# One-core hybrid decoder block: PSUM banks of scores and transposes, the first weight transfer, and the place of the diagonal products

## The chip, the core and the metric

The kernel runs on one core of a Trainium2 chip. The metric is the device time of one execution in microseconds (us); the time given for a kernel is the median of several runs. Engines are named as the profile names them: PE (TensorE matmul), PEld (TensorE weight load), DVE (VectorE), ACT (ScalarE), POOL (GpSimd), SP (SyncE, which here only issues DMAs).

## What is computed

For x of 256 tokens by 1024 channels the reference computes one decoder block:

```python
h = rmsnorm(x, attn_norm_g)
hq, hf, hi, hg, aq, ak, av, gl = split(h @ w_in)          # 1024 x 9216
y_hg = hgrn2_mix(hq, hf, hi, hg, lb, hg_out_norm_g) @ w_branch_hg
att  = moba_attention(rmsnorm(aq), rmsnorm(ak), av, rel_bias_table)
y_at = att @ w_branch_attn
merged = sigmoid(gl[0]) * y_hg + sigmoid(gl[1]) * y_at
x = x + merged @ w_out
h2 = rmsnorm(x, ffn_norm_g)
x = x + (silu(h2 @ w_ffn_gate) * (h2 @ w_ffn_up)) @ w_ffn_down
```

With 256 tokens and blocks of 256 the attention is plain causal attention of 8 heads of 128 with a relative bias. The recurrence (8 heads of 128) is computed by the kernel as a masked product of queries and decayed keys.

## The kernel before, in words

**Precision.** Each large product is made from three matmuls in the type fp32r: an operand is split into a high part (`whi`, cast on ACT, L55) and a remainder (`wlo`, subtraction on DVE, L56), and the kernel sums high x high, high x low and low x high (L81 to L83, L98 to L101, L608 to L610). So each weight tile needs a DMA issued by SP (L64), an ACT cast and a DVE subtraction before PE can use both parts. Transposes, scores and the products of the recurrence are in plain fp32.

**Start (L116 to L161).** The first product, V0, is the first half of the recurrence's values. Its weights and x come in seven pieces, one k-tile of 128 rows each and two in the last. For a piece, ACT casts the weights (L146), DVE or ACT multiplies x by the norm gain held in `vec` (L150 for the first k-tile, L152 for the others), DVE makes the two remainders (L153, L155), and PE does six matmuls per k-tile (L160). Before: the weights of the first k-tile (256 KB) and then `vec` (17.5 KB) are issued by ACT (L120, L121), all the other transfers by SP, of which x of the first k-tile (128 KB) leads (L122). The eight matmuls of L129 on a tile of ones run in the meantime.

**Blocks.** `feat_block` (L86) and `tok_block` (L76) make 512 output columns each, from two chunks of four k-tiles of weights. Three buffers of `wraw`, `whi` and `wlo` turn round; SP issues the next load when DVE has read a `wraw` for the last time.

**PSUM.** There are eight banks in three groups: `pw` has four (the blocks), `pa` two, `ph` two. Before the change, the transposes in `head_T` (L424 to L434) and the scores (L450 to L461) take `pa` alone. The recurrence's levels (L322) take `ph`, and so do its diagonal products (L309).

**Attention and recurrence (L498 to L535).** They are written interleaved: a block of k or q, then one level of the recurrence, and so on. A level (`hgrn_level`) is an ACT copy (L320), a group of small matmuls into one `ph` bank (L332), four predicated copies out of it on DVE (L338) and DVE products (L349, L351) that the next level needs. `hgrn_diag` (L297) makes three passes over 128x2048 elements on DVE (L301, L302, L56) and a cast on ACT (L55); `hgrn_diag_put` (L306) multiplies the result by ones on PE and puts it on the diagonal of A.

**What sets the order.** Program order is only a priority: when the program is built, a planner places the instructions of each engine by it and by its own model of when operands and buffers are ready, and the engine then runs that fixed order. This can be seen in the trace, where pieces of a level (L332) stand between the transposes of `head_T` (L431), which come before it in the program.

Of the kernel before, what the change touches and what calls it, by code (L numbers as in the profile page):

```python
# [14 lines left out]
P = 128  # L15
# [12 lines left out]
def tile_hgrn2_moba_block(ctx: ExitStack, tc: tile.TileContext, xm, xT, vecs, table, onehot,  # L28
                          w_in, w_hg, w_at, w_out, w_gate, w_up, w_down, out):
    nc = tc.nc  # L30
# [10 lines left out]
    def ph(name="ph"):  # L41
        return psum.tile([P, 512], F32, name=name, tag="ph", bufs=2)

    def pa(name="pa"):
        return psum.tile([P, 512], F32, name=name, tag="pa", bufs=2)
# [8 lines left out]
    def split(src, hi, lo):  # L54
        nc.scalar.copy(hi, src)  # L55
        nc.vector.tensor_sub(lo, src, hi.bitcast(F32))  # L56
# [19 lines left out]
    def tok_block(w, c0, act, parts=(4, 4), bank=pw):  # L76
        ps = [bank(), bank()]
        for kt, wh, wl in chunks(w, c0, 512, parts):
            for tb in range(2):
                ts = slice(tb * P, (tb + 1) * P)  # L80
                nc.tensor.matmul(ps[tb], part(act, kt, 0)[:, ts], wh, start=(kt == 0), stop=False)  # L81
                nc.tensor.matmul(ps[tb], part(act, kt, 0)[:, ts], wl, start=False, stop=False)  # L82
                nc.tensor.matmul(ps[tb], part(act, kt, 1)[:, ts], wh, start=False, stop=(kt == KT - 1))  # L83
        return ps
# [32 lines left out]
    xTr = big.tile([P, KT, S], F32, name="xTr", tag="T1")  # L117
    XT = [big.tile([P, 4, 2, S], F32R, name=f"XT{i}", tag=("XH", "XL")[i]) for i in range(2)]
    raws = [wp.tile([P, 4, 512], F32, name="wraw") for _ in range(2)]
    nc.scalar.dma_start(raws[0][:, 0, :], w_in[0:P, 2048:2560])  # L120
    nc.scalar.dma_start(vec, vecs)  # L121
    nc.sync.dma_start(xTr[:, 0:1, :], xT[:, 0:1, :])  # L122
    ones = const.tile([P, P], F32, name="ones")
    nc.vector.memset(ones, 1.0)
# [55 lines left out]
    def rinv(dst, ss, n):  # L180
        nc.vector.tensor_scalar(dst, ss, 1.0 / n, EPS, op0=OP.mult, op1=OP.add)
        nc.scalar.activation(dst, dst, AF.Sqrt)
        nc.vector.reciprocal(dst, dst)
# [41 lines left out]
    def put_tok(dst, ps, half):  # L225
        for tb in range(2):
            nc.scalar.mul(dst[:, tb, half * 512:(half + 1) * 512], ps[tb], rx[:, tb:tb + 1])
# [31 lines left out]
    bank = pa()  # L259
# [37 lines left out]
    def hgrn_diag():  # L297
        qk = big.tile([P, 2, H, P], F32, name="qk", tag="T9")
        qkh = big.tile([P, 2, H, P], F32R, name="qkh", tag="T10")
        qkl = big.tile([P, 2, H, P], F32R, name="qkl", tag="T8")  # L300
        nc.vector.tensor_mul(qk, Q, K)  # L301
        nc.vector.tensor_mul(QA, Q, Fg)  # L302
        split(qk, qkh, qkl)
        return qkh, qkl

    def hgrn_diag_put(qkh, qkl):  # L306
        for tb in range(2):
            for g in range(2):
                bank = ph().rearrange("p (h t) -> p h t", h=4)  # L309
                for m, part in enumerate((qkh, qkl)):  # L310
                    nc.tensor.matmul(bank, ones_r, part[:, tb, 4 * g:4 * g + 4, :], start=(m == 0), stop=(m == 1))
                nc.vector.tensor_mul(A[:, tb, 4 * g:4 * g + 4, :], bank,
                                     ident.unsqueeze(1).to_broadcast([P, 4, P]))
# [103 lines left out]
    def qk_block(tok, sq, c0, half, bank=pw):  # L417
        put_tok(tok, tok_block(w_in, c0 + half * 512, XT, bank=bank), half)
        for tb in range(2):
            for h in range(half * 4, half * 4 + 4):  # L420
                jk = small.tile([P, P], F32, name="jk")
                nc.scalar.activation(jk, tok[:, tb, h * P:(h + 1) * P], AF.Square, accum_out=sq[:, tb, h:h + 1])

    def head_T(tok, tag, nm, gain):  # L424
        tT = big.tile([P, H, S], F32, name=nm, tag=tag)
        for g in range(4):
            bank = pa()
            for i in range(2):
                for tb in range(2):
                    h = 2 * g + i  # L430
                    nc.tensor.transpose(bank[:, i * S + tb * P:i * S + (tb + 1) * P],  # L431
                                        tok[:, tb, h * P:(h + 1) * P], ident)
            nc.scalar.mul(tT[:, 2 * g:2 * g + 2, :].rearrange("p h t -> p (h t)"), bank, gain)
        return tT  # L434

    def keys(ktok, kss):
        rk = small.tile([P, 2, H], F32, name="rk")
        rinv(rk, kss, P)
        for tb in range(2):
            kv = ktok[:, tb, :].rearrange("p (h d) -> p h d", h=H)  # L440
            nc.vector.tensor_mul(kv, kv, rk[:, tb, :].unsqueeze(2).to_broadcast([P, H, P]))
        return head_T(ktok, "T9", "kT", kg)

    def scores(qtok, qss, kT):
        rq = small.tile([P, 2, H], F32, name="rq")
        rinv(rq, qss, P)
        qT = head_T(qtok, "T10", "qT", qg[:, 0:1])
        S0 = big.tile([P, H, P], F32, name="S0", tag="T13")
        S1 = big.tile([P, H, S], F32, name="S1", tag="T7")
        for sc, tb, w, bt in ((S0, 0, P, B0), (S1, 1, S, B1)):  # L450
            m = 512 // w
            for g in range(H // m):
                bank = pa()
                for i in range(m):
                    h = m * g + i
                    nc.tensor.matmul(bank[:, i * w:(i + 1) * w], qT[:, h, tb * P:(tb + 1) * P], kT[:, h, 0:w],  # L456
                                     start=True, stop=True)
                for i in range(m):
                    h = m * g + i
                    nc.vector.scalar_tensor_tensor(sc[:, h, :], bank[:, i * w:(i + 1) * w], rq[:, tb, h:h + 1],  # L460
                                                   bt[:, h, :], op0=OP.mult, op1=OP.add)  # L461
        return S0, S1
# [35 lines left out]
    ktok = big.tile([P, 2, D], F32, name="ktok", tag="T7")  # L498
    kss = small.tile([P, 2, H], F32, name="kss")
    qk_block(ktok, kss, 5120, 0, bank=pa)  # L500
    qkd = hgrn_diag()
    qk_block(ktok, kss, 5120, 1)
    hgrn_diag_put(*qkd)
    hgrn_level(0)
    qtok = big.tile([P, 2, D], F32, name="qtok", tag="T8")
# [5 lines left out]
    hgrn_level(2)  # L511
    put_tok(V, tok_block(w_in, 2048 + 512, XT), 1)
    S0, S1 = scores(qtok, qss, kT)
    hgrn_level(3)
    Va = big.tile([P, 2, D], F32, name="Va", tag="T8")
# [37 lines left out]
    for half in range(2):  # L553
# [5 lines left out]
        for tb in range(2):  # L559
            g = G[0][:, tb, hs]  # L560
            nc.vector.tensor_mul(g, g, ps[tb])
            nc.vector.tensor_add(g, g, G[1][:, tb, hs])
            bank = ph()
# [8 lines left out]
    for half in range(2):  # L572
        ps = tok_block(w_out, half * 512, M)
        for tb in range(2):
            xs = x2[:, tb, half * 512:(half + 1) * 512]
            nc.vector.tensor_add(xs, xs, ps[tb])
            bank = ph()
# [110 lines left out]
```

## Time and profile before

| | us |
|---|---|
| median of 3 runs | 508.66 |
| lowest and highest | 508.34, 509.21 |
| profiled execution | 509.63 |
| span of its records | 507.6 |
| PE busy in it | 499.4 (98%) |

The profile is of one execution, which took 509.63 us; its engine records span 507.6 us, so 2.03 us lie outside of them. Times in rows are counted from the start of the span. In a timeline row the first number is the start, the second the length, then come the engine, the line, the operation, the tiles and the count; brackets name what ended an idle time before the row. Consecutive matmuls overlap in the records, so the distance between starts is what a matmul costs the engine.

### The profile page before, as it was taken

The page shows a single profiled execution, that of the slowest core. Times are in us where ns is not written, and L with a number is a line of the kernel's source. Part 1 is how long each engine was busy: PE and PEld are TensorE (multiplying, and loading weights), DVE is VectorE, ACT ScalarE, POOL GpSimd, SP SyncE. Part 2 cuts the span into 40 slices and gives each one's busy share as a digit, 9 for nine tenths or more (in the row PEclk, how much of TensorE's full clock was granted, in tenths as well). Part 3 has the DMA queues.
Part 4 walks back from the last instruction along what each step waited for, and adds up shares of the span by engine and source line. Part 5 has one row for each costly group of instructions (what it writes and reads, how often), then busy time and mean ns, then how long its engine had stood idle before and what let it go on. Part 6 is the DMA issues. An engine that isn't in the chain of part 4 may idle for free.

```text
span 507.6 us, 6636 instructions
## 1 busy us (share of the span) xinstructions
PE 499.4 (98%) x2674; PEld 419.4 (83%) x2674; DVE 332.7 (66%) x380; ACT 283.3 (56%) x418; POOL 21.3 (4%) x41
## 2 busy tenths in 40 slices
PE   7999999999999999999999999999999999999996
PEld 6878887788888888888888888888888888888885
DVE  5669998887599643373456577867655746566372
ACT  5497566777658656955434334665535535544350
POOL 9201300000000000000000000000000000000000
PEclk9999999999999999999999999999999999999999
DMA  8956956524523642276556555556655655653522
GB/s 245 388 178 193 338 197 224 190 83 167 167 70 112 235 166 86 80 252 224 188 168 221 187 170 166 167 175 201 203 167 175 212 194 169 202 169 90 190 94 83
DMA packets 44126, 91.20 MB, mean 180 GB/s; under 512 B 1944, under 2 KB 5048, under 8 KB 44096
## 3 DMA queue, kind: packets, MB, share of 16 engines
q1 hardware_dynamic: 43072, 87.86, 51.8%
q0 software_dynamic: 736, 2.65, 1.7%
q8 instruction: 21, 0.34, 0.3%
q10 hardware_dynamic: 288, 0.28, 0.2%
q14 instruction: 9, 0.07, 0.0%
HBM read 89.70 MB, written 1.07 MB: 179 GB/s over the span
## 4 chain that ended last, share of the span: by engine, by line
PE 95%; ACT 2%; DMA 1%; DVE 1%; issue 0%; DVEq 0%; ACTq 0%
PE pw L99 21%; PE pw L81 13%; PE pw L82 13%; PE pw L83 13%; PE pw L98 9%; PE acc L608 4%; PE acc L609 4%; PE acc L610 4%; PE pw L160 3%; PE ph L332 2%; PE pw L101 1%; PE pa L456 1%; DMA vec<-vecs 1%; PE ph L382 1%; PE pa L492 1%; PE pa L81 1%
## 5 line engine op out<-in xcount | busy, mean ns | idle before, releaser
L56 DVE TENSOR_TENSOR wlo<-wraw,whi 128x2048 fp32r<-128x2048 f32 (+1 forms) x83 | 182.2, 2197 | 113.6 <-ACT whi L55 113.2
L55 ACT CAST whi<-wraw 128x2048 fp32r<-128x2048 f32 (+1 forms) x83 | 151.7, 1829 | 114.4 <-PE pw L83 52.7
L99 PE MATMUL pw<-x2T,whi 128*128 128x512 f32 x352 | 121.8, 398 | 0.0
L98 PE MATMUL pw<-x2T,wlo 128*128 128x256 f32 x308 | 86.5, 281 | 0.0
L81 PE MATMUL pw<-whi,XT 128*128 128x512 f32 x192 | 76.0, 396 | 0.0
L82 PE MATMUL pw<-wlo,XT 128*128 128x512 f32 x192 | 75.4, 392 | 0.6 <-DVE wlo L56 0.6
L83 PE MATMUL pw<-whi,XT 128*128 128x512 f32 x192 | 75.2, 392 | 0.0
L99 PEld LDWEIGHTS pw<-x2T,whi 128*128 128x128 f32 x352 | 63.4, 188 | 12.4
L98 PEld LDWEIGHTS pw<-x2T,wlo 128*128 128x128 f32 x308 | 58.2, 189 | 1.8
L99 PE MATMUL pw<-XT,whi 128*128 128x512 f32 x128 | 44.5, 399 | 0.2 <-DVE Fg L111 0.2
L82 PEld LDWEIGHTS pw<-wlo,XT 128*128 128x128 f32 x192 | 36.1, 188 | 8.2 <-DVE wlo L56 1.0
L81 PEld LDWEIGHTS pw<-whi,XT 128*128 128x128 f32 x192 | 36.1, 188 | 7.5
L83 PEld LDWEIGHTS pw<-whi,XT 128*128 128x128 f32 x192 | 36.1, 188 | 7.4
L608 PE MATMUL acc<-whi,hT 128*128 128x512 f32 x88 | 34.3, 390 | 0.0
L610 PE MATMUL acc<-whi,hT 128*128 128x512 f32 x88 | 34.3, 389 | 0.0
L609 PE MATMUL acc<-wlo,hT 128*128 128x512 f32 x88 | 34.2, 389 | 0.0
L98 PE MATMUL pw<-XT,wlo 128*128 128x256 f32 x112 | 31.4, 280 | 0.0
L99 PEld LDWEIGHTS pw<-XT,whi 128*128 128x128 f32 x128 | 23.3, 188 | 5.1 <-DVE Fg L111 0.5
L98 PEld LDWEIGHTS pw<-XT,wlo 128*128 128x128 f32 x112 | 21.1, 189 | 0.6
L610 PEld LDWEIGHTS acc<-whi,hT 128*128 128x128 f32 x88 | 16.5, 188 | 3.5
L609 PEld LDWEIGHTS acc<-wlo,hT 128*128 128x128 f32 x88 | 16.5, 188 | 3.5
L608 PEld LDWEIGHTS acc<-whi,hT 128*128 128x128 f32 x88 | 16.5, 188 | 3.3
(217 smaller groups left out, 689.4 us busy)
## 6 DMA issues: line engine op xcount, KB each, us to landing
wraw<-w_in SPq DMA_DIRECT2D x32, 1024.0 KB, 5.3
wraw<-w_down SPq DMA_DIRECT2D x11, 1024.0 KB, 4.9
wraw<-w_gate SPq DMA_DIRECT2D x10, 1024.0 KB, 5.1
wraw<-w_up SPq DMA_DIRECT2D x10, 1024.0 KB, 5.1
wraw<-w_at SPq DMA_DIRECT2D x4, 1024.0 KB, 5.1
wraw<-w_hg SPq DMA_DIRECT2D x4, 1024.0 KB, 5.1
wraw<-w_out SPq DMA_DIRECT2D x4, 1024.0 KB, 5.1
wraw<-w_in SPq DMA_DIRECT2D x5, 512.0 KB, 8.2
```

Source lines behind the costliest of these rows:

```text
L55: nc.scalar.copy(hi, src)
L56: nc.vector.tensor_sub(lo, src, hi.bitcast(F32))
L81: nc.tensor.matmul(ps[tb], part(act, kt, 0)[:, ts], wh, start=(kt == 0), stop=False)
L82: nc.tensor.matmul(ps[tb], part(act, kt, 0)[:, ts], wl, start=False, stop=False)
L83: nc.tensor.matmul(ps[tb], part(act, kt, 1)[:, ts], wh, start=False, stop=(kt == KT - 1))
L98: nc.tensor.matmul(ps[ct][:, 0:S], lo[:, i, cs], part(act, kt, 0), start=False, stop=False)
L99: nc.tensor.matmul(ps[ct], hi[:, i, cs], both, start=(kt == 0), stop=(kt == KT - 1))
L160: nc.tensor.matmul(V0[tb], part(XT, kt, am)[:, tb * P:(tb + 1) * P], w[:, i, :], start=(kt == 0 and am == 0 and w is wh), stop=(kt == KT - ...
L332: nc.tensor.matmul(o, KP[:, h, qs], t, start=True, stop=True)
L608: nc.tensor.matmul(acc[tb][half], act[:, j, 0, ts], hi[:, i, cs], start=st, stop=False)
L609: nc.tensor.matmul(acc[tb][half], act[:, j, 0, ts], lo[:, i, cs], start=False, stop=False)
L610: nc.tensor.matmul(acc[tb][half], act[:, j, 1, ts], hi[:, i, cs], start=False, stop=en)
```

## The change

Four edits. (1) The weights of the first k-tile are issued by SP, ahead of everything else there, and ACT issues `vec` alone. (2) `head_T` takes its four banks from `pa` and `ph` in turn. (3) So do the groups of scores. (4) `hgrn_diag()` is called after the second block of k, not between the two.

```diff
     raws = [wp.tile([P, 4, 512], F32, name="wraw") for _ in range(2)]
-    nc.scalar.dma_start(raws[0][:, 0, :], w_in[0:P, 2048:2560])
     nc.scalar.dma_start(vec, vecs)
+    nc.sync.dma_start(raws[0][:, 0, :], w_in[0:P, 2048:2560])
     nc.sync.dma_start(xTr[:, 0:1, :], xT[:, 0:1, :])
...
     def head_T(tok, tag, nm, gain):
         tT = big.tile([P, H, S], F32, name=nm, tag=tag)
         for g in range(4):
-            bank = pa()
+            bank = (pa, ph)[g % 2]()
...
             for g in range(H // m):
-                bank = pa()
+                bank = (pa, ph)[g % 2]()
...
     qk_block(ktok, kss, 5120, 0, bank=pa)
+    qk_block(ktok, kss, 5120, 1)
     qkd = hgrn_diag()
-    qk_block(ktok, kss, 5120, 1)
     hgrn_diag_put(*qkd)
```

## Rows read from the trace of the kernel before

**Rows 1.** The page: busy time by engine, and the chain that ended last by engine.

```profile
PE 499.4 (98%) x2674; PEld 419.4 (83%) x2674; DVE 332.7 (66%) x380; ACT 283.3 (56%) x418; POOL 21.3 (4%) x41
...
PE 95%; ACT 2%; DMA 1%; DVE 1%; issue 0%; DVEq 0%; ACTq 0%
```

**Rows 2.** The chain that ended last, first 21 us: start, length, what.

```profile
0.81 0.41 ACTq L120
...
1.24 4.71 DMA vec<-vecs
...
6.05 0.55 DVE XT L150
...
6.75 14.24 PE pw L160 x48
```

**Rows 3.** DMA issues of the start and two others: KB each, us from issue to landing.

```profile
wraw<-w_in ACTq DMA_DIRECT2D x1, 256.0 KB, 4.2
xTr<-xT SPq DMA_DIRECT2D x1, 128.0 KB, 3.9
...
vec<-vecs ACTq DMA_DIRECT2D x1, 17.5 KB, 4.7
...
line_d<-line POOLq DMA_DIRECT2D x1, 24.0 KB, 2.1
```

**Rows 4.** Waits of the SP queue: us in total, times, longest.

```profile
SPq L142 <- DMA wraw<-w_in: 1.5, 1, 1.5
```

**Rows 5.** First product: timeline of PE, matmuls of L160, and the page's granted clock.

```profile
8.88 1.91 PE L160 MATMUL pw<-whi,XT 128*128 128x512 f32 x4
10.58 1.05 PE L160 MATMUL pw<-wlo,XT 128*128 128x512 f32 x2
...
13.55 1.09 PE L160 MATMUL pw<-whi,XT 128*128 128x512 f32 x4
...
L160 PE MATMUL pw<-whi,XT x32: 389/389/764, 6.7 to 20.6; 128*128 128x512 f32 x32
...
PEclk9999999999999999999999999999999999999999
```

**Rows 6.** Timeline, 5 to 20 us: casts of the weights, remainder of the next block's.

```profile
5.03 1.35 ACT L146 CAST whi<-wraw 128x512 fp32r<-128x512 f32 x2 [1.81 <-DMA wraw<-w_in]
...
17.16 2.57 DVE L56 TENSOR_TENSOR wlo<-wraw,whi 128x1024 fp32r<-128x1024 f32 x2 [1.02 <-ACT whi L55]
17.41 1.06 ACT L55 CAST whi<-wraw 128x1024 fp32r<-128x1024 f32 x1 [0.29 <-DMA wraw<-w_in]
```

**Rows 7.** Timeline of PE, DVE and ACT around the second block of k, 68 to 80 us.

```profile
68.18 1.92 ACT L55 CAST whi<-wraw 128x2048 fp32r<-128x2048 f32 x1
...
70.62 2.29 DVE L301 TENSOR_TENSOR qk<-Q,K 128x2048 f32<-128x2048 f32 x1
...
77.23 4.49 DVE L56 TENSOR_TENSOR wlo<-wraw,whi 128x2048 fp32r<-128x2048 f32 x2
...
78.61 0.39 PE L81 MATMUL pw<-whi,XT 128*128 128x512 f32 x1
79.57 0.50 PE L82 MATMUL pw<-wlo,XT 128*128 128x512 f32 x1 [0.57 <-DVE wlo L56]
```

**Rows 8.** Timeline of PE where transposes and a level alternate, 104 to 136 us.

```profile
105.59 1.04 PE L332 MATMUL ph<-QA,KP 128*64 128x64 f32 x28
...
107.62 0.50 PE L81 MATMUL pw<-whi,XT 128*128 128x512 f32 x1
...
132.24 0.56 PE L332 MATMUL ph<-QA,KP 128*64 128x64 f32 x10
...
134.96 0.50 PE L81 MATMUL pw<-whi,XT 128*128 128x512 f32 x1
```

**Rows 9.** The chain that ended last: four transposes, and a level in one piece.

```profile
108.35 0.44 PE pa L431 x4
119.24 1.08 PE ph L332 x32
```

**Rows 10.** Timeline of DVE: the copies that empty a level's bank.

```profile
107.74 2.70 DVE L338 COPY_PREDICATED A<-mask,ph 64x256 f32<-64x256 uint32 x4 [1.75 <-PE ph L332]
```

## The prediction

> **What bounds the kernel now.** I read the page first. PE is busy for 98% of the span and makes up 95% of the chain that ended last [rows 1]. PE's own work is not touched by this change: no matmul is added or removed. So the change can only pay where PE stands still or runs slowly, and I looked for these places by comparing the starts of neighbouring PE rows over the whole timeline. Three groups of them lie where the edits are.
>
> The first is the start. The chain of waits runs through the transfer of `vec`: issued at 1.24 us behind the first weights on ACT's queue, under way for 4.71 us, then the scaling of x (0.55 us), and only at 6.75 us the first matmul of V0 [rows 2]. The weights' cast had begun at 5.03 us [rows 6], and x of the first k-tile, issued at about 0.81 us, had landed 3.9 us later, at 4.7 us [rows 3]. So `vec` comes last, by about a microsecond.
>
> The second is the beginning of k's second block. PE's first matmul there starts at 78.61 us, the next only at 79.57 us, when `wlo` arrives [rows 7]. The weights' high part had been there since 68.18 + 1.92 = 70.10 us, but DVE began three passes for the diagonal products at 70.62 us, 2.29 us or so each, and came to `wlo` at 77.23 us [rows 7].
>
> The third is where transposes of k and q (L431) cut a level's matmuls (L332) into pieces [rows 8].
>
> **The change part by part.**
>
> *First transfers (edit 1).* `vec` moves from second to first on ACT's queue, so it leaves at 0.81 instead of 1.24 us. What it then takes is not shown: not less than the 2.1 us of a transfer of similar size on an almost empty queue, not more than the 4.7 us of now [rows 3]. That is landing at 2.9 to 5.5 us. I take a value near 4.5, since the large transfers still run beside it; it is then no longer the last. The weights go to SP's head at the same instant as before, 0.81 us, and should land as before after 4.2 us or a little less, at 5.0 us [rows 3]; with half of the two casts' 1.35 us behind it [rows 6], PE can't start before about 5.7 us, a gain of at most 1.05 us. x of the first k-tile goes back by one issue, 0.43 us (the distance of ACT's two issues [rows 2]). With its present 3.9 us it lands at 1.24 + 3.9 = 5.14 us; if standing behind 256 KB costs it what it cost `vec`, 4.7 us, at 5.95 us, when `vec` lands now [rows 2, 3]. The gain is between 0.8 and 0 us. The pair of 384 KB is the same as now and landed complete at 5.0 us, so I keep near the first end: x at 5.25 us, a gain of 0.7 us, first matmul at about 6.05 us.
>
> Everything else on SP is also moved back one place, 0.43 us: six more pieces of weights and x, and behind them the next block's weights. What covers it: SP stood for 1.5 us at L142 waiting for the first weights to land [rows 4], and the transfers are limited by their rate, not their issue. [...]
>
> [...]
>
> [...]
>
> Nor can the gain be larger than the next block allows. Its first remainders are finished at 17.16 + 2.57 = 19.73 us, and they hang on a cast that waited for its transfer until 17.41 us [rows 6]. PE needs the third of those four k-tiles some 0.7 us after it enters the block (two k-tiles, each a matmul of 512 columns, 0.23 us, and one of 256, taken as half of that), so it could enter at 19.73 - 0.7 = 19.05 us. It does so at about 20.6 us: V0's matmuls end at 6.75 + 14.24 = 20.99 us [rows 2], and the last one's 0.39 us overlap with what follows. The cap is 1.55 us. Behind it the long weights wait for buffers that DVE frees in step with PE, so what is won stays won.
>
> *Diagonal products (edit 4).* The stall from 78.61 to 79.57 us is 0.96 us for one matmul of 0.23 us: 0.73 us lost, and 0.1 us more in the slow first matmul after it (0.50 us against 0.39) [rows 7]. With the products behind the block in priority, DVE can take `wlo` at 70.6 us, when its high part is ready, and be done at 72.9 us, 5.7 us ahead of PE. Even if two of the three passes still came first, `wlo` would end at 70.62 + 3 x 2.29 = 77.5 us, in time. The products' results are needed by PE only after the block (48 matmuls of 0.23 us, 11 us, from 78.6 us), so 6.9 us of DVE and one cast on ACT lie beside it. Gain 0.83 us, between 0 (order unchanged) and 0.85.
>
> *Banks (edits 2 and 3).* No work changes. With two banks the third transpose group waits for ACT to empty the first, and the planner fills in pieces of a level. From 105.59 to 107.62 us lie 32 level records and 4 transposes: 2.03 us. In one piece the level takes 1.08 us, and four transposes 0.44 us [rows 8, 9], so the cutting costs 0.51 us. From 132.24 to 134.96 us it is the same with 8 transposes: 2.72 - 1.08 - 0.88 = 0.76 us. With four banks the 16 transposes can go in one piece, and the level too. At best 1.27 us are won. At worst the level, which needs a `ph` bank itself, is cut elsewhere, and as much is lost. I take 0.5 us, less than half of the best, since the level's bank now has to be shared. The scores stand between main matmuls now, with hardly any loss beyond their own work; zero for them.
>
> **Sum.** 0.7 + 0.83 + 0.5 = 2.03 us. Against the profiled execution's own 509.63 us that gives 507.6. This execution was 0.97 us above the median of 508.66, so the forecast for the median is 508.66 - 2.03 = 506.6 us.
>
> **The rivals.**
>
> *One, slower: the `ph` banks turn into the wait.* A level's bank is not free when its matmuls end; DVE empties it with four copies of 2.70 us, after a wait [rows 10]. PE runs in a fixed order: if a transpose or score group stands behind such a bank, PE waits for up to 2.7 us, once at k's transposes, once at q's and once at the scores: up to 8.1 us, less what the planner foresees. From 2.0 us of such waiting on, the whole gain is gone; at two full waits, 5.4 us, the time is 508.7 - 1.5 + 5.4 = 512.6 us (the 0.5 us of the banks not counted). For it: levels and transposes are next to each other in the program. Against it: the blocks' matmuls need neither group of banks and are there to be placed in between, as they are now [rows 8]. Chance 0.1.
>
> *Two, no change that can be told: only one part works.* The planner goes by its own model, so it may still cut the levels; and x, put back by one place, may land at 5.95 us, so that the start stays. Only the stall goes: 508.66 - 0.83 = 507.8 us. If the products too stayed ahead, it would be 508.7 us. For it: two of my three terms rest on bounds that reach to zero. Chance 0.18.
>
> [...] Chance 0.15.
>
> **How the numbers follow.** The forecast, 506.6 us, has 0.57. About 0.2% (1.0 us) is what a measurement of this kernel can tell from no change. The forecast and rival three are faster than that: 0.72; rival two is the same: 0.18; rival one is slower: 0.10. The range goes from 505.2 us, the cap of the start with the best case of the banks (508.66 - 1.55 - 0.83 - 1.0), to 508.5 us, which takes in rival two nearly whole; what is left out is rival one and the far ends.
>
> **What would show it.** Right: `vec` lands before x, the first V0 matmul starts near 6 us, matmuls with 0.23 us between them begin clearly before 12 us; `wlo` of k's second block ends several us before its L82, which follows its L81 after 0.23 us; the levels of L332 stand in one piece. Wrong: the first V0 matmul still waits until 6.7 us; a PE row in the second block of k that waits for DVE; PE rows that wait for L338, L433 or L460 to free a bank.

## The result, and the profile after

The changed kernel took 505.31 us (median of 5; 505.06 to 506.59) against 508.66 us; the ratio is 0.994, with a 95% interval from 0.9924 to 0.9956, so 2.2 to 3.9 us less. Its profiled execution took 506.59 us, the slowest of the five. Between the two profiled executions the gain is 509.63 - 506.59 = 3.04 us.

Two lines of the page of the changed kernel (against [rows 1]):

```profile
span 504.5 us, 6639 instructions
...
PE 496.2 (98%) x2674; PEld 417.0 (83%) x2674; DVE 332.9 (66%) x380; ACT 283.0 (56%) x418; POOL 20.4 (4%) x41
```

PE does as many instructions as before. Where the time went can be read by the starts of the same PE instruction in the two timelines:

| PE instruction | before | changed | earlier by |
|---|---|---|---|
| first matmul of V0 (L160) | 6.75 | 4.91 | 1.84 |
| first matmul of the next block (L99) | 20.83 | 19.29 | 1.54 |
| first L81 of k's second block | 78.61 | 77.24 | 1.37 |
| its L82 | 79.57 | 77.47 | 2.10 |
| level 2 (L332) | 119.17 | 116.64 | 2.53 |
| level 4 (L332) | 151.42 | 148.29 | 3.13 |
| first transposes of the branches' sum (L565) | 272.75 | 269.64 | 3.11 |

In this pair of executions about 1.4 us come from the start, 0.9 from k's second block (the difference is 2.27 us from the level behind it on), 0.26 from k's transposes and 0.6 from the stretch with q's transposes and the scores. Nothing is given back after that.

The start's 1.4 us are a difference of two executions, not the price of the edit. The first L81 of k's second block came between 77.38 and 78.66 us in the four profiled executions that have the start of before (the table's, and e2, e3 and e7 below), and between 75.61 and 77.24 us in four with the edited start (the table's, and e0, e1 and e8). Both executions of the table lie near the late end of their group. The other terms repeat to a few hundredths from trace to trace.

**The start.** DMA issues of the changed kernel (KB each, us to landing), which answer to [rows 3]:

```profile
wraw<-w_in SPq DMA_DIRECT2D x1, 256.0 KB, 3.0
vec<-vecs ACTq DMA_DIRECT2D x1, 17.5 KB, 3.1
...
xTr<-xT SPq DMA_DIRECT2D x1, 128.0 KB, 2.9
```

All three took 3 us or so, the first two from 0.81 us, x from 1.25 us. The PE timeline (against [rows 5]) and the chain that ended last, first 21 us (start, length, what; against [rows 2]):

```profile
4.91 0.70 PE L160 MATMUL pw<-whi,XT 128*128 128x512 f32 x2
...
7.69 0.73 PE L160 MATMUL pw<-whi,XT 128*128 128x512 f32 x2 [1.04 <-ACT XT L152]
...
8.72 1.07 PE L160 MATMUL pw<-whi,XT 128*128 128x512 f32 x4
...
16.05 0.73 PE L160 MATMUL pw<-whi,XT 128*128 128x512 f32 x2 [1.26 <-ACT XT L152]
```

```profile
2.65 4.93 DMA wraw<-w_in
...
7.61 6.91 DMA wraw<-w_in
...
14.54 1.05 ACT whi L146
...
15.62 1.24 DVE wlo L155
...
16.90 2.55 PE pw L160 x10
```

V0's matmuls start at two distances in these traces: 0.425 us in the row of before at 8.88 us (1.70 us for four) and 0.23 us in its row at 13.55 us, (1.09 - 0.389) / 3 [rows 5]; the latter is the prediction's 0.23 us for a matmul. Here they are called, in this order, the lower and the higher level. The granted clock is 1.00 in both stretches, so it does not tell them apart; where an expectation says clock, these levels are meant. Before, each engine's busy time in the two stretches, then the granted clock, the DMA engines' busy share and GB/s:

```profile
8.88:10.58 1.70, 1.70 (x5) 1.32 (x4) 1.70 (x4) 1.24 (x3) 1.70 (x4) 1.00 0.82 283
13.55:14.41 0.86, 0.86 (x5) 0.72 (x4) 0.82 (x3) 0.13 (x1) 0.86 (x3) 1.00 0.99 353
```

V0 now begins at 4.91 us and runs at the higher level (0.23 us per matmul at 8.72 us), but it stands twice for its inputs: the chain no longer passes through `vec` but through the last weights, 6.91 us under way and issued at 7.61 us, when by the chain the third k-tile's weights had landed. In this execution the start has turned from PE-bound (held by PE's own matmuls once V0 had begun) to transfer-bound.

**The diagonal products.** DVE in the changed kernel, 69 to 80 us, and PE at k's second block (against [rows 7]):

```profile
69.24 2.29 DVE L301 TENSOR_TENSOR qk<-Q,K 128x2048 f32<-128x2048 f32 x1
71.45 2.28 DVE L56 TENSOR_TENSOR wlo<-wraw,whi 128x2048 fp32r<-128x2048 f32 x1
73.65 2.28 DVE L302 TENSOR_TENSOR QA<-Q,Fg 128x2048 f32<-128x2048 f32 x1
75.85 2.28 DVE L56 TENSOR_TENSOR wlo<-wraw,whi 128x2048 fp32r<-128x2048 f32 x1
78.05 2.28 DVE L56 TENSOR_TENSOR qkl<-qk,qkh 128x2048 fp32r<-128x2048 f32 x1
```

```profile
77.24 0.39 PE L81 MATMUL pw<-whi,XT 128*128 128x512 f32 x1
77.47 0.39 PE L82 MATMUL pw<-wlo,XT 128*128 128x512 f32 x1
```

The planner did not put `wlo` first, as I had it, but second: one pass of the products still precedes it. It ends at 73.73 us, 3.7 us before PE asks for it, and the stall is gone.

**The banks.** PE in the changed kernel, transposes, scores and levels (against [rows 8]):

```profile
102.35 0.60 PE L431 MATMUL pa<-ident,ktok 128*128 128x128 f32 x4
102.79 0.60 PE L431 MATMUL ph<-ident,ktok 128*128 128x128 f32 x4
...
105.35 1.16 PE L332 MATMUL ph<-QA,KP 128*64 128x64 f32 x32 [0.17 <-ACT kT L433]
...
130.49 1.06 PE L456 MATMUL pa<-kT,qT 128*128 128x128 f32 x8
...
135.14 1.03 PE L456 MATMUL ph<-kT,qT 128*128 128x256 f32 x4
136.33 1.15 PE L332 MATMUL ph<-QA,KP 128*64 128x64 f32 x32
```

Transposes and scores go through in groups without a main matmul between them, and the levels in this stretch are one piece of 32 records each. The wait of rival one exists, at 105.35 us, and is 0.17 us long.

### The profile page after: what moved, and what is told of

Same layout as the page of the kernel before. It is cut to its first block, busy times and chain, and to the rows that moved or that the text cites. A ratio compares the mean times of both kernels' runs of the same rounds, so it can differ in the third digit from the quotient of the medians.

```text
span 504.5 us, 6639 instructions
## 1 busy us (share of the span) xinstructions
PE 496.2 (98%) x2674; PEld 417.0 (83%) x2674; DVE 332.9 (66%) x380; ACT 283.0 (56%) x418; POOL 20.4 (4%) x41
## 3 DMA queue, kind: packets, MB, share of 16 engines
HBM read 89.70 MB, written 1.07 MB: 180 GB/s over the span
## 4 chain that ended last, share of the span: by engine, by line
PE 93%; DMA 2%; ACT 2%; DVE 1%; SPq 0%; issue 0%; DVEq 0%
PE pw L99 21%; PE pw L81 13%; PE pw L82 13%; PE pw L83 13%; PE pw L98 9%; PE acc L610 4%; PE acc L608 4%; PE acc L609 4%; DMA wraw<-w_in 2%; PE ph L332 2%; PE pw L101 1%; PE ph L382 1%; PE pa L492 1%; PE pa L81 1%; PE pa L82 1%; PE pa L83 1%
## 5 line engine op out<-in xcount | busy, mean ns | idle before, releaser
L99 PE MATMUL pw<-x2T,whi 128*128 128x512 f32 x352 | 121.9, 398 | 0.0
L98 PE MATMUL pw<-x2T,wlo 128*128 128x256 f32 x308 | 86.5, 281 | 0.0
L81 PE MATMUL pw<-whi,XT 128*128 128x512 f32 x192 | 75.8, 395 | 0.0
L82 PE MATMUL pw<-wlo,XT 128*128 128x512 f32 x192 | 75.2, 392 | 0.0
L99 PEld LDWEIGHTS pw<-x2T,whi 128*128 128x128 f32 x352 | 63.5, 188 | 12.5
L98 PEld LDWEIGHTS pw<-x2T,wlo 128*128 128x128 f32 x308 | 58.2, 189 | 1.8
L99 PE MATMUL pw<-XT,whi 128*128 128x512 f32 x128 | 44.7, 399 | 0.2 <-DVE Fg L111 0.2
L81 PEld LDWEIGHTS pw<-whi,XT 128*128 128x128 f32 x192 | 36.1, 188 | 7.5
L82 PEld LDWEIGHTS pw<-wlo,XT 128*128 128x128 f32 x192 | 36.1, 188 | 7.3
L98 PE MATMUL pw<-XT,wlo 128*128 128x256 f32 x112 | 31.5, 281 | 0.0
L99 PEld LDWEIGHTS pw<-XT,whi 128*128 128x128 f32 x128 | 23.3, 188 | 5.1 <-DVE Fg L111 0.5
L98 PEld LDWEIGHTS pw<-XT,wlo 128*128 128x128 f32 x112 | 21.2, 189 | 0.8
```

The source lines that it names most:

```text
L98: nc.tensor.matmul(ps[ct][:, 0:S], lo[:, i, cs], part(act, kt, 0), start=False, stop=False)
L99: nc.tensor.matmul(ps[ct], hi[:, i, cs], both, start=(kt == 0), stop=(kt == KT - 1))
```

## The experiments

Each kernel was compared with the kernel before, run alongside on the same chip. Where the changed kernel is the measure, it is its repetition (505.56 us), on the same chip too except for the last experiment.

**The edits one by one.** The first three kernels are the kernel before with one part of the diff shown ahead: edit 1, edit 4, and edits 2 and 3.

> Theory (three separate places, gains add up): V0 starts at about 4.9 us at full speed, the next block begins 1.4 to 1.5 us earlier than before, and the whole time falls by 1.4 us, to about 507.3 us; the stall before L82 of k's second block stays, 0.7 us. Rival (the edits only work together, since what the start wins is waited for again at the stall behind the diagonal products): under 0.5 us.

Measured: 507.46 us against 508.32 us, ratio 0.9985 (0.9972 to 0.9999).

> Theory: the stall of 0.73 us and the slow matmul after it go, nothing else moves: 0.8 to 0.9 us less, about 507.8 us. Rival (moving three DVE passes back makes a later remainder late): the PE row that waits for DVE turns up between 80 and 95 us and the gain is under 0.4 us.

Measured: 507.48 us, ratio 0.9986 (0.9977 to 0.9994). In the profile the shift (how much earlier than before the same instruction starts) grows from 1.24 us to 2.08 us across the stall and is 2.12 us from k's transposes on, so 0.84 to 0.88 us are the edit's; the rest of the shift is another start.

> Theory: levels 1 and 2 run in one piece and the transposes in one piece; the shift grows by 0.3 us at k's transposes and by 0.6 us at q's and the scores: 0.9 us less in all, about 507.8 us. Rival (the gain there came from the shifted start, which gave the planner another order): the levels stay cut and the gain is under 0.3 us.

Measured: 507.79 us, ratio 0.9985 (0.9975 to 0.9995). The shift grows from 1.16 to 1.41 us at k's transposes and to 1.99 us after the scores: 0.83 us.

Each part is worth some 0.5 to 0.9 us by the medians, 2.2 us together, and each is faster by itself. The start's edit is the least certain: its interval reaches almost to no change, and its twelve runs lie between 505.88 and 508.85 us, those of the products' edit between 506.98 and 508.73 us. Its profiled execution, 506.69 us, is among the faster ones: there the first L81 of k's second block came 3.0 us earlier than before.

> The changed kernel once more, unedited, for comparison within one session. Theory (the three places add up): 0.75 to 1.4 us from the start, 0.8 from the stall, 0.8 from the banks: 2.4 to 3.0 us less than before. Rival (the parts help each other, so that the sum is more than the parts, which were 0.8, 0.7 and 0.8 us): over 3.2 us less.

Measured: 505.56 us against 508.40 us, ratio 0.9946 (0.9934 to 0.9959): 2.84 us less. That is within what the parts give with their intervals, and the rival's 3.2 us is not reached. But the first measurement, 3.35 us, passes it, so whether the parts help each other by some tenths stays open. In this execution the next block's first matmul comes at 17.89 us, not 19.29, with the same program.

**Is it PE's higher level?** The kernel before with more warming matmuls, then the changed one with fewer:

```diff
-    for _ in range(8):
+    for _ in range(12):     # e4;  16 in e11;  2 in e6
         nc.tensor.matmul(warm[:, 0:P], ones, ones, start=True, stop=True)
```

> Kernel before with 12 instead of 8 warming matmuls, so that PE has no pause before V0, whose inputs still come at 6.7 us. Theory (the start's gain is the clock's: PE never pauses between the warming matmuls and V0): V0's matmuls have 0.23 us between them from its first on, though it starts no earlier; 0.8 to 1.5 us less. Rival (the gain is the earlier transfers): V0 starts at 6.7 us, still at 0.425 us per matmul, and the time is that of before within 0.3 us.

Measured: 507.23 us against 508.32 us, ratio 0.9977 (0.9967 to 0.9988). The one profiled execution, 509.39 us, is the slowest of the twelve, so it doesn't show what most of them did:

```profile
7.26 0.70 PE L160 MATMUL pw<-whi,XT 128*128 128x512 f32 x2 [1.24 <-DVE gm L196]
8.47 1.07 PE L160 MATMUL pw<-wlo,XT 128*128 128x512 f32 x2 [0.51 <-DVE wlo L155]
```

PE still paused before V0, from the end of the warming matmuls at 6.02 to 7.26 us. V0's first two matmuls were at the higher level (0.70 us for both); PE then waited again, and the next two, from 8.47 us, were at the lower (1.07 us for both).

> The kernel before with 16 warming matmuls, which last until V0's inputs are there. Theory (before, V0 was bound by PE at its lower level; the changed kernel has room for that level, this one hasn't): V0's matmuls have 0.23 us between them nearly from the first, its end comes 1 to 1.5 us earlier, and the time falls by 0.8 to 1.5 us without any transfer being moved. Rival (the transfers alone set the end of V0): within 0.3 us of before.

Measured: 507.34 us against 508.38 us, ratio 0.9983 (0.9974 to 0.9991), all runs within 0.63 us. PE timeline of its start:

```profile
1.13 6.29 PE L129 MATMUL warm<-ones 128*128 128x128 f32 x32 [1.13 <-DVE ones L124]
7.17 0.71 PE L160 MATMUL pw<-whi,XT 128*128 128x512 f32 x2
...
8.19 1.08 PE L160 MATMUL pw<-whi,XT 128*128 128x512 f32 x4
```

There was no pause; V0 ran at the higher level from its start, and the next block began at 18.17 us, 2.66 us earlier than before. Only 1.30 us of it were left at 67 us: PE waits for DVE at L98, L190 and L101 on the way, 1.3 us together by its waits. And the stall at k's second block was gone too, since DVE reached the diagonal products 2.43 us earlier and PE its block only 1.3 us earlier. So this kernel shows that PE's level bound V0 before, but its 1.04 us can't be taken as the higher level's price, since the stall's share is in it.

> The changed kernel with 2 instead of 8 warming matmuls, so that PE pauses for about 2.5 us before V0. Theory (the start's gain hangs on PE being at the higher level when V0 begins): V0 starts near 4.9 us but at 0.425 us per matmul for several us, the end of V0 comes later, and the time rises by 0.7 to 1.5 us against the changed kernel. Rival (V0 is held by its transfers, whose last piece lands at about 14.5 us, so the clock does not matter): within 0.3 us of the changed kernel.

Measured: 505.46 us against 505.56 us for the changed kernel. PE timeline of its start:

```profile
4.90 1.19 PE L160 MATMUL pw<-whi,XT 128*128 128x512 f32 x2 [2.55 <-DVE XT L150]
...
6.74 1.91 PE L160 MATMUL pw<-whi,XT 128*128 128x512 f32 x4
...
9.30 1.42 PE L160 MATMUL pw<-whi,XT 128*128 128x512 f32 x4
```

V0 runs at the lower level (0.425 us per matmul) until 9.3 us or later, and by the medians it costs nothing. The theory falls: V0 begins just as early, so its start comes from the earlier transfers. The rival's forecast holds, though not all of its reason: in this execution V0 doesn't wait for a piece any more, and the next block begins at 18.29 us, between the 17.89 and 19.29 us of the two executions with eight warming matmuls. By these traces, what the lower level costs V0 would otherwise have spent standing for its last pieces.

**Which half of edit 1?**

```diff
-    nc.scalar.dma_start(raws[0][:, 0, :], w_in[0:P, 2048:2560])
     nc.scalar.dma_start(vec, vecs)
+    nc.scalar.dma_start(raws[0][:, 0, :], w_in[0:P, 2048:2560])
```

> The kernel before with vec ahead of the first weights, both still issued by ACT. Theory (what held V0 was vec behind 256 KB; who issues the weights matters little): vec lands at 3.9 us or so as in the changed kernel, V0 starts near 5.2 us, and the time falls by 0.5 to 1.0 us, as with the start's edit alone. Rival (the weights must lead SP's queue): the weights land later than 5 us, V0 starts at 6 us or after, under 0.4 us.

Measured: 508.04 us against 508.38 us, ratio 0.9996 (0.9986 to 1.0006). ACT's timeline:

```profile
5.58 1.14 ACT L146 CAST whi<-wraw 128x512 fp32r<-128x512 f32 x2 [2.36 <-DMA wraw<-w_in]
```

`vec` landed after 3.0 us, but the weights, second on ACT's queue, were there only for a cast at 5.58 us, and V0 began at 6.25 us. That is what the rival said: the wait has moved from `vec` to the weights. The interval overlaps that of the start's edit, so the medians alone don't separate the two. Nor does V0's start alone decide: this profiled execution, 506.99 us, is the fastest of its eleven, V0 ran at the higher level nearly from its first matmul, and the next block began at 17.58 us.

**Transposes or scores?** Edit 2 alone (`head_T`):

> The kernel before with the banks of the transposes of q and k alone in turn, the scores still on one pair. Theory (what is won is that levels are no longer cut by transposes): shift of 0.25 us at k's transposes and 0.4 to 0.6 at q's, as with all banks. Rival (the scores' banks do the larger part, since with two banks the scores are spread between main matmuls): 0.25 us at k's and under 0.3 us from there to the end.

Measured: 508.86 us against 508.38 us, ratio 1.0006 (0.9994 to 1.0017). PE timeline at q's transposes and the scores, and the pieces of level 5:

```profile
132.79 2.22 PE L456 MATMUL pa<-kT,qT 128*128 128x128 f32 x16
134.93 0.80 PE L332 MATMUL ph<-QA,KP 128*64 128x64 f32 x18
135.66 1.13 PE L456 MATMUL pa<-kT,qT 128*128 128x256 f32 x4
136.72 0.57 PE L332 MATMUL ph<-QA,KP 128*64 128x64 f32 x12
137.22 1.99 PE L456 MATMUL pa<-kT,qT 128*128 128x256 f32 x8
139.14 0.33 PE L332 MATMUL ph<-QA,KP 128*64 128x64 f32 x2
...
159.48 0.80 PE L332 MATMUL ph<-QA,KP 128*64 128x64 f32 x20
...
166.30 0.56 PE L332 MATMUL ph<-QA,KP 128*64 128x64 f32 x10
...
167.82 0.33 PE L332 MATMUL ph<-QA,KP 128*64 128x64 f32 x2
```

At k's transposes 0.26 us are won, and from there to 185 us 0.6 us are lost. Some 0.2 us of that go at q's transposes and the scores: the transposes are through earlier, and now the scores, on two banks, cut the level into three pieces. The other 0.4 us go between 151 and 185 us, where the transposes of the probabilities, also on two banks, cut level 5 into three pieces instead of two. The theory falls; the rival's under 0.3 us is met, but neither said that it would be a loss. The cut moves to the next groups that are short of banks. Edit 2 pays only together with edit 3; edit 3 alone was not run.

**Further along the same lines.** From the changed kernel: the transposes of the probabilities and the products with the values on all four banks, then x in larger transfers, then both.

```diff
-                bank = pa().rearrange("p (h t) -> p h t", h=4)      # probs_T
+                bank = (pa, ph)[g % 2]().rearrange("p (h t) -> p h t", h=4)
...
-            bank = pa()                                             # values
+            bank = (pa, ph)[g % 2]()
```

> The changed kernel with the transposes of the probabilities and the products with the values also taking banks from both pairs. Theory (a level cut in pieces costs 0.1 to 0.15 us at each change of kind): level 5's matmuls go in one piece and level 6's too; about 0.5 us less than the changed kernel. Rival (those groups wait for ACT and DVE to empty the banks, not for banks): no difference over 0.2 us.

Measured: 504.55 us, 1.0 us less than the changed kernel; its six runs (503.75 to 505.50 us) overlap with those of the changed kernel (504.89 to 506.10 us). Against the changed kernel's first profile the shift grows by 0.74 us between 150 and 195 us. PE timeline:

```profile
161.25 0.60 PE L481 MATMUL ph<-ident,S 128*128 128x128 f32 x4
161.95 1.15 PE L332 MATMUL ph<-QA,KP 128*64 128x64 f32 x32
```

Level 5 is in one piece, and so is level 6, with 32 records from 181.42 us; in the changed kernel each was in two.

```diff
-            nc.sync.dma_start(xTr[:, xs, :], xT[:, xs, :])
+            if k0 % 2 == 1 and k0 < 5:
+                nc.sync.dma_start(xTr[:, k0:k0 + 2, :], xT[:, k0:k0 + 2, :])
+            elif k0 == 5:
+                nc.sync.dma_start(xTr[:, 5:8, :], xT[:, 5:8, :])
```

> The changed kernel with x of k-tiles 1 to 7 in three transfers (two, two and three k-tiles) instead of six. Theory (from 6 us on the start is bound by the transfers, and pieces of 1 KB per row move more slowly than larger ones): the next block begins 0.5 to 1 us earlier, 0.5 to 1 us less than the changed kernel. Rival (V0's first k-tiles wait for more bytes at once, or the transfers' rate doesn't hang on the piece): 0 to 0.5 us more.

Measured: 504.79 us, 0.8 us less, all five runs within 0.26 us. DMA in the stretch from 10 to 12 us (last two columns: share, GB/s), first in the changed kernel's repetition, then here:

```profile
10.00:12.00 2.00, 2.00 (x11) 1.62 (x10) 2.00 (x5) 1.45 (x4) 2.00 (x5) 1.00 0.88 326
```

```profile
10.00:12.00 2.00, 2.00 (x11) 1.65 (x9) 2.00 (x5) 1.60 (x4) 2.00 (x5) 1.00 1.04 408
```

The rate rises to 408 GB/s, and the DMA engines are busy throughout. In the same stretch it was 264 GB/s in the changed kernel's first profile and 354 GB/s in e1, and 407 GB/s in the kernel of the next experiment. In the changed kernel's first profile the six pieces of x with 1 KB per row (128 KB) took 4.8 us each in the median, and the six of weights with 2 KB per row (256 KB) 4.9 us: for each byte the smaller ones took about twice as long from issue to landing. Whether the longer rows, the fewer issues on SP, or the next block's weights that follow them sooner (from 7.38 us instead of 8.29) do it, these runs don't tell apart.

> The changed kernel with both steps that paid: x in three larger transfers, and all banks in turn for the probabilities' transposes and the values. Theory (they lie at different places and add up): 1.5 us less than the changed kernel, about 503.9 us. Rival (the start is bound elsewhere by now): 504.5 us, no better than the more banks alone.

Measured: 504.16 us against 508.38 us for the kernel before, ratio 0.9918 (0.9905 to 0.993), 1.4 us less than the changed kernel, of 1.0 and 0.8 us for the two steps apart. So most of both adds up; this beats both kernels of the study.

## Why the prediction was right, and where its steps were off

The direction and the range held (505.31 us in 505.2 to 508.5), but at the range's edge: I had 2.03 us, and 3.35 us were measured by the medians, 3.04 us between the profiled executions, 2.84 us in the repetition. The three places were the right ones. That the first measurement still fell inside the range was in part luck: the lower end was added up as the cap of the start with 1.0 us for the banks, whose best case I had put at 1.27 us, and that sum is 505.28, not 505.2.

- *First transfers, 0.7 us.* Mis-sized: V0 began 1.84 us earlier (4.91 us, not 6.05), outside the cap of 1.05 us. The step that failed is "should land as before after 4.2 us or a little less". The weights took 3.0 us and x 2.9 us, against the 4.2 and 3.9 us that I carried over from rows in which both had been issued at the same instant on two queues. `vec`, 3.1 us, was within its bounds. Of the 1.84 us, 1.4 were left at k's block. What the edit is worth in the median is less sure: 0.86 us were measured for it alone; the whole gain of 2.84 to 3.35 us less the 1.76 us of the other two places leaves 1.1 to 1.6 us, an estimate.
- *SP's queue one place back.* The sum has no term for it, and that failed for V0's pieces. That the transfers were limited by their rate fits the trace of before: from 2 to 14 us the DMA engines' busy share of each 2 us was 0.87 to 1.03, at 227 to 340 GB/s. The second k-tile's weights took 4.9 us, and PE stood for 1.04 us at 7.69 us. The last weights were issued at 7.61 us against 7.30 before, but their cast could begin only at 14.54 us against 12.64 before, and PE stood for 1.26 us at 16.05 us. In the repetition that cast began at 12.56 us, and PE stood for 0.45 us. So a part of the earlier start is given back, and how much differs from run to run.
- *The cap of 1.55 us.* The next block came 1.54 us earlier in the profiled execution, which fits by chance: with the same program it came at 17.89 us in the repetition. The transfer on which the cap rested is no fixed time, and two of its readings were off. PE entered the next block at 20.83 us before, not at about 20.6, which is the start of V0's last matmul; and PE's order comes to the third k-tile's remainder 1.39 us after the entry (20.83 to 22.22 us), not 0.7 us, since it takes up a second group of columns first. By the prediction's own rule the cap would have been about 2.5 us.
- *PE's two levels.* No run shows the ground of the 0.15 for rival three, a start worth the whole cap; what the runs showed in its place is this. The level was decisive before the change (16 warming matmuls: V0 at 0.23 us per matmul from its start and 1.04 us less, the stall's share included) and no longer after it: two warming matmuls, with V0 at 0.425 us per matmul until 9.3 us or later, gave the same time as eight (505.46 and 505.56 us). At which level V0 starts differs between executions of one program: in the changed kernel 4.91 us shows two matmuls in 0.70 us, in its repetition two in 1.19 us. What sets it is not shown.
- *Diagonal products, 0.83 us.* Right: 0.84 to 0.88 us with the edit alone, 0.90 us in the whole. DVE's order was another than I had it, but within the case that I had costed (passes before `wlo` that still leave time).
- *Banks, 0.5 us.* Mis-sized: 0.86 us in the profile, 0.83 us there with edits 2 and 3 alone (0.53 us by the medians). Counting each group by itself, with zero for the scores, failed: with edit 2 alone the level that the transposes no longer cut was cut by the scores, and nothing was gained, so after q's transposes the gain needs the scores' banks too. The best case of 1.27 us was not reached; a level in one piece is still entered and left.
- *Rival one* (waits for `ph`): no wait behind L338; the one PE row that waits for a copy out of a transposes' bank, ACT's at L433, stands for 0.17 us. *Rival two* (one part only) did not occur; each part alone was faster than before.

## What to carry to other kernels

When one engine is busy all the time, look for its lost time in the starts of neighbouring instructions, place by place; here three places of 0.8 to 1.4 us each, by the traces, added up, and a place that is mended may move its wait to the next group that lacks the same thing (banks), so mend the row of them together. At a kernel's start, look at which transfer of the first product lands last, and don't stop when it is mended: here the wait went from `vec` to the weights when `vec` alone was moved, and to the last pieces when both were. And don't price such a change from one profile, since one program's start differs from run to run by as much as the change is worth (1.40 us between two executions of the changed kernel, against 0.86 us for the start's edit alone).

## What was unexpected of the hardware

- The same 256 KB took 2.9 to 3.2 us as the first transfer of SP's queue (seven traces), 3.6 to 4.7 us as the first of ACT's (six) and 4.3 us as the second of ACT's (one); 17.5 KB took 3.0 to 3.3 us when first on ACT's queue and 4.3 to 5.2 us behind the weights. Position alone doesn't explain it: x took 3.3 to 4.4 us as the first of SP's queue with the weights issued on ACT's at the same instant, and 2.9 to 3.1 us as the second, right behind the weights. The cause stays open.
- One program's start differs by more than a microsecond from run to run: the next block began at 19.29 and at 17.89 us in two executions of the changed kernel. With x in larger transfers the five runs lay within 0.26 us.
- 32 level records cost PE 1.08 us in one piece, and more when they are cut: in the changed kernel a piece of 10 records between two groups of transposes took 0.49 us (161.36 to 161.85 us), 0.15 us more than 10 of 32 in one piece, an estimate from these two numbers.
